# A two-layer decoder trunk in single-pass float32: part of the second MLP product as seven block products for eight

## The chip, the cores and the metric

One core of a Trainium2 chip runs the kernel. The metric is the device time of one execution in microseconds (us), the median of the runs shown. The program before takes 853.79 us.

## What is computed

The reference is a decoder trunk of two layers on 256 tokens of width 1024. Each layer has a mixer (sparse attention and retention), a squared-ReLU MLP and a gated embedding. What the change touches is the MLP:

```
h = rmsnorm(x, norm_mlp[i])
x = x + jnp.square(jax.nn.relu(h @ w_ff1[i])) @ w_ff2[i]
gate = jax.nn.sigmoid(rmsnorm(x, norm_ple[i]) @ w_ple_gate[i])
x = x + gate * (p[i] @ w_ple[i])
```

`w_ff1` is 1024 x 4096 and `w_ff2` is 4096 x 1024.

## The kernel before

The residual stays on the chip as `XT`, features on partitions, tokens along the free axis (8 chunks of 128 features x 256 tokens). Every float32 product is made of three TensorE passes on float32r operands: each operand is split in a rounded part ("high") and the remainder ("low"), and high x high, high x low and low x high are added in PSUM (`three`, L485).

Weights come in units of 128 x 1024 (512 KB). `PLAN` (`_plan`, L71) is the order of units; `take` (L360) hands out the next one and has `advance` (L331) start loads on the SP queue and splits four units ahead. A split (`unit_split`, L312) is one rounding copy on ScalarE (`hi`) and one subtraction on VectorE (`lo`); there are six `hi` and six `lo` buffers (`HL`), so a unit's split waits until TensorE is through with the unit six places before it. TensorE's order is that of the code; ScalarE's, VectorE's and the SP queue's is made by a scheduler from dependences and priorities. Each of these queues runs in order.

The MLP of a layer (L1078 to L1135) works in 16 pairs of contraction tiles, 256 rows of the hidden width each. For a pair `i`, the first product (`ff1_unit`, `b_unit`, L490) takes two units, weights stationary and 256 tokens moving: 48 matmuls of 256 columns into one PSUM tile of the pool `mm` (three banks, L122). `ff1_end` (L1089) makes Relu, its square twice (one rounded, for the high part) and the remainder: two ScalarE and two VectorE instructions of 512 columns. Two pairs later the second product (`ff2`, L1103, with `wide`, L509) takes two units of `w_ff2`, weights stationary again: 2 tiles x 8 output blocks x 3 passes = 48 matmuls of 256 columns into four PSUM accumulators (pools `sc` and `pt`, two banks each). The norm's factor `r` is left out of the MLP's input; its square, spread over partitions by two flips (`finish_b`, L469), multiplies the sums at the end (L1132), which are then added to `XT` and fed to the next stage (`feed`, L454: `XH` on ScalarE, `XL` on VectorE, squares for the norm).

After the MLP comes the product `ple` (two units, 24 matmuls each of 256 columns for two halves), which needs nothing of the MLP, and then the gate product (`gate`), which needs `XH` and `XL`.

A flip (`flip`, L222) is a 128 x 128 transposition on TensorE against an identity.

Of the kernel before, what the change touches and what calls it, by code (L numbers as in the profile page):

```python
# [70 lines left out]
def _plan(l):  # L71
    r = [({"w": "w1"}.get(n, n), u) for n, u in SEQ[l] if n not in ("fa", "fb", "sq")]
    for n in ("ma", "mb"):
        r += [(n, u) for u in range(8)]
    r += [("ua", u) for u in range(4)] + [("ub", 0), ("ub", 1), ("ub", 2), ("out", 0), ("out", 1)]
    r += [("ub", 3)] + [("out", u) for u in range(2, 8)]
    r += [("ff1", u) for u in (0, 2, 1, 3)]
    for i in range(14):
        r += [("ff1", 2 * i + 4), ("ff1", 2 * i + 5), ("ff2", 2 * i), ("ff2", 2 * i + 1)]
    r += [("ff2", u) for u in range(28, 32)]  # L80
# [7 lines left out]
BIG_UNITS = [x for x in PLAN if x[1] != "kvg"]  # L88
# [6 lines left out]
def trunk(ctx: ExitStack, tc: tile.TileContext, xT, wu, wg, cst, msk, par, pin, out):  # L95
# [25 lines left out]
    def mm_tile(shape):  # L121
        return ps.tile(shape, F32, tag="mm", name=nm("mm"), bufs=3)  # L122
# [16 lines left out]
    def big(shape, tag, name, dt=F32):  # L139
        return bp.tile(shape, dt, tag=tag, name=nm(name))  # L140
# [39 lines left out]
    def fresh(t=None):  # L180
        cur[0] = vt["pe"] if t is None else t
# [107 lines left out]
    state = {"load": 0, "split": 0, "take": 0}  # L289
    raws, his, los, spans, due = {}, {}, {}, {}, {}  # L290

    def unit_load(i):
        key = PLAN[i]
        if key[1] == "w1":
            t = bp.tile([P, NW], F32, tag=f"B{(1, 2, 5, 6)[key[2] % 4]}", name=f"raw{i}")
        else:
            t = wp.tile([P, NW], F32, tag="raw", name=f"raw{i}", bufs=RAW)
        if key[1] == "kvg":
            nc.sync.dma_start(t[:, :560], wg[KVG_IX[key]])
            spans[i] = 560  # L300
        else:
            src = wu[BIG_IX[key]]
            if i == 0:
                for c in range(4):
                    load_x(c, c + 1)
                    nc.sync.dma_start(t[:, c * 256:(c + 1) * 256], src[:, c * 256:(c + 1) * 256])
            else:
                nc.sync.dma_start(t, src)
            spans[i] = NW
        raws[i] = t  # L310

    def unit_split(i, ahead=None):  # L312
# [12 lines left out]
        due[i] = cur[0]

    ring = [0]
    for key in PLAN:
        ring.append(ring[-1] + (key[1] != "w1"))

    def advance(i):  # L331
        n = len(PLAN)
# [189 lines left out]
    def layer(l, st):  # L522
# [550 lines left out]
        ph = big([P, 2, S], "S7", "ph", F32R)  # L1073
        pl = big([P, 2, S], "S8", "pl", F32R)
        act(ph, pT, AF.Copy)
        sub(pl, pT, ph.bitcast(F32))

        def ff1_unit(i, u):  # L1078
            if u == 0:
                ff[i] = mm_tile([P, 2, S])  # L1080
            b_unit(ff[i], take(l, "ff1", 2 * i + u), XH, XL, 4 * u, u == 0, u == 1)
            if u == 1:
                ff1_end(i, ff[i])

        def ff1(i):
            for u in range(2):
                ff1_unit(i, u)

        def ff1_end(i, pm):  # L1089
            fresh()  # L1090
            au = big([P, 2, 2, S], f"B{i % 3}", "au")
            ho = big([P, 2, 2, S], f"B{3 + i % 4}", "ho", F32R)
            a, u2 = au[:, 0], au[:, 1]
            h, o = ho[:, 0], ho[:, 1]
            act(a, pm, AF.Relu)
            tt(out=h, in0=a, in1=a, op=ALU.mult)
            act(u2, a, AF.Square)
            sub(o, u2, h.bitcast(F32))
            ff[i] = (h, o)

        pf = []

        def ff2(i):  # L1103
            h, o = ff.pop(i)
            for u in range(2):
                w = take(l, "ff2", 2 * i + u)
                if not pf:
                    pf.extend(accumulators())
                for n in range(4):
                    wide(pf[n], w, n, h[:, u, :], o[:, u, :], i == 0 and u == 0, False)  # L1110

        ff1_unit(0, 0)
        ff1_unit(1, 0)
        ff1_unit(0, 1)
        ff1_unit(1, 1)
        finish_a(stf)
        ff1(2)
        finish_b(stf, square=True)
        ff2(0)
        for i in range(1, 14):  # L1120
            ff1(i + 2)
            ff2(i)
        ff2(14)
        stp = new_stage(l, 2)
        ws = [take(l, "ff2", 30 + u) for u in range(2)]
        dz = [big([P, 2, 2, S], f"B{1 + i}", "dz") for i in range(2)]
        h, o = ff.pop(15)
        for n in range(4):
            for u in range(2):
                wide(pf[n], ws[u], n, h[:, u, :], o[:, u, :], False, u == 1)  # L1130
            d = dz[n // 2][:, n % 2]
            tt(out=d, in0=pf[n], in1=bc2(stf["RB"]), op=ALU.mult)  # L1132
            xc = XT[:, 2 * n:2 * n + 2, :]
            tt(out=xc, in0=xc, in1=d, op=ALU.add)
            feed(stp, 2 * n)  # L1135
# [108 lines left out]
def _unit(l, name, u, a):  # L1244
# [27 lines left out]
        return bform(a["w_up_ret"][l], 256 * u, 0, 4)  # L1272
    if name == "out":
        return a["w_out"][l][u * P:(u + 1) * P]
    if name == "ff1":
        return bform(a["w_ff1"][l], 256 * (u // 2), 4 * (u % 2), 4)
    if name == "ff2":
        return a["w_ff2"][l][u * P:(u + 1) * P]
    if name == "gate":
# [45 lines left out]
```

## Time and profile before

| | |
|---|---|
| median of three runs | 853.79 us (853.41 to 854.06) |
| the profiled execution | 853.69 us, span 851.9 us |
| TensorE busy | 840.6 us, 99% |
| VectorE busy | 605.1 us, 71% |
| ScalarE busy | 499.8 us, 59% |
| GpSimd busy | 77.5 us, 9% |
| bytes moved | 152.11 MB, mean 179 GB/s |

The span runs from the first to the last instruction of the profiled execution; the device time is 1.8 us more. Busy times of engines overlap. Matmuls are pipelined: one takes longer from its start to its modelled end than the next one's start is away.

### The profile page before, as it was taken

What the parts mean: (1) busy time and instruction counts of PE and PEld (TensorE: products, weight loads), DVE (VectorE), ACT (ScalarE), POOL (GpSimd) and SP (SyncE); (2) the same over time, 40 slices, a digit from 0 to 9 for tenths busy, and PEclk for the clock granted to TensorE, in tenths of its full rate; (3) what the DMA queues carried; (4) which work ended last, traced back from release to release, by engine and by line L of the source; (5) the groups of instructions that cost most, each with busy time, mean ns of one, the idle gap of its engine ahead of it and who ended that gap; (6) DMA issues with size and microseconds to landing.
All of it is one profiled execution on the core that took longest, in us unless ns stands there. A gap on an engine that the chain in (4) does not pass through costs nothing.

```text
span 851.9 us, 16528 instructions
## 1 busy us (share of the span) xinstructions
PE 840.6 (99%) x6647; PEld 816.6 (96%) x6647; DVE 605.1 (71%) x977; ACT 499.8 (59%) x836; POOL 77.5 (9%) x68
## 2 busy tenths in 40 slices
PE   8999999999999999999999999999999999999997
PEld 7988899999999999999999989999999999999997
DVE  6897897786955555557789979886877555555584
ACT  6786877544744545445567768765465444444471
POOL 1240241000000000000004104120000000000000
PEclk9999999999999999999999999999999999999999
DMA  8877454356565655556655664443546556656541
GB/s 262 311 243 242 127 154 126 121 166 188 175 185 187 180 191 179 192 180 221 200 193 158 218 198 141 133 138 121 175 149 216 181 189 183 189 183 187 185 124 50
DMA packets 44284, 152.11 MB, mean 179 GB/s; under 512 B 5168, under 2 KB 6960, under 8 KB 44208
## 3 DMA queue, kind: packets, MB, share of 16 engines
q1 hardware_dynamic: 44064, 151.04, 55.9%
q8 instruction: 52, 0.85, 0.4%
q14 instruction: 24, 0.20, 0.1%
q10 hardware_dynamic: 144, 0.01, 0.0%
HBM read 149.99 MB, written 1.05 MB: 177 GB/s over the span
## 4 chain that ended last, share of the span: by engine, by line
PE 89%; DVE 6%; DMA 1%; ACT 1%; issue 1%; POOL 1%; SPq 0%; DVEq 0%; ACTq 0%
PE mm L220 51%; PE sc L220 18%; PE pt L220 14%; PE ot L220 4%; PE pt L225 2%; DVE lo L192 2%; DMA raw<-in_wu_dram 1%; POOL rso L214 1%; DVE tmp L200 0%; ACT hi L188 0%; DVE zt L192 0%; ACT tmp L188 0%; DVE yss L204 0%; DVE T L200 0%; DVE zs L192 0%
## 5 line engine op out<-in xcount | busy, mean ns | idle before, releaser
L192 DVE TENSOR_TENSOR lo<-raw,hi 128x1024 fp32r<-128x1024 f32 (+2 forms) x287 | 347.6, 1217 | 185.7 <-ACT hi L188 184.9
L188 ACT ACTIVATE hi<-raw 128x1024 fp32r<-128x1024 f32 (+2 forms) x287 | 296.5, 1039 | 276.6 <-PE mm L220 158.7
L220 PE MATMUL mm<-XH,hi 128*128 128x256 f32 x992 | 283.5, 286 | 0.0
L220 PE MATMUL mm<-XH,lo 128*128 128x256 f32 x992 | 279.6, 282 | 0.0
L220 PE MATMUL mm<-XL,hi 128*128 128x256 f32 x992 | 279.1, 281 | 0.0
L220 PEld LDWEIGHTS mm<-XH,hi 128*128 128x128 f32 x992 | 187.0, 188 | 2.0
L220 PEld LDWEIGHTS mm<-XL,hi 128*128 128x128 f32 x992 | 187.0, 189 | 1.7
L220 PEld LDWEIGHTS mm<-XH,lo 128*128 128x128 f32 x992 | 186.8, 188 | 0.0
L220 PE MATMUL sc<-ho,hi 128*128 128x256 f32 x512 | 96.8, 282 | 0.0
L220 PE MATMUL pt<-ho,hi 128*128 128x256 f32 x512 | 96.6, 281 | 0.0
L220 PEld LDWEIGHTS pt<-ho,hi 128*128 128x128 f32 x512 | 78.6, 188 | 0.0
L220 PEld LDWEIGHTS sc<-ho,hi 128*128 128x128 f32 x512 | 78.5, 188 | 0.0
L220 PE MATMUL pt<-ho,lo 128*128 128x256 f32 x256 | 72.0, 281 | 0.0
L220 PE MATMUL sc<-ho,lo 128*128 128x256 f32 x256 | 72.0, 281 | 0.0
L220 PEld LDWEIGHTS sc<-ho,lo 128*128 128x128 f32 x256 | 48.2, 188 | 0.0
L220 PEld LDWEIGHTS pt<-ho,lo 128*128 128x128 f32 x256 | 48.2, 188 | 0.0
L214 POOL TENSOR_TENSOR e<-e,acf 128x512 f32<-128x512 f32 (+1 forms) x32 | 37.3, 1194 | 113.4 <-DVE acf L192 76.0
L220 PE MATMUL mm<-hi,XH 128*128 128x512 f32 (+2 forms) x128 | 44.3, 346 | 0.0
L220 PE MATMUL mm<-lo,XH 128*128 128x512 f32 (+2 forms) x128 | 43.7, 342 | 0.1
L220 PE MATMUL mm<-hi,XL 128*128 128x512 f32 (+2 forms) x128 | 43.7, 341 | 0.0
L188 ACT ACTIVATE e<-e,nmx 128x128 f32<-128x128 f32 (+2 forms) x96 | 37.6, 394 | 7.4 <-DVE nmx L208 7.4
L214 POOL TENSOR_TENSOR r<-ms,mhalf 128x2 f32<-128x2 f32 x6 | 6.6, 1100 | 365.2 <-DVE ms L196 337.0
(192 smaller groups left out, 1362.7 us busy)
## 6 DMA issues: line engine op xcount, KB each, us to landing
raw<-in_wu_dram SPq DMA_DIRECT2D x275, 512.0 KB, 3.7
raw<-in_wg_dram SPq DMA_DIRECT2D x8, 280.0 KB, 4.2
cst<-in_cst_dram SPq DMA_DIRECT2D x1, 768.0 KB, 7.0
out_dram<-XT SPq DMA_DIRECT2D x3, 256.0 KB, 2.4
XT<-in_xT_dram SPq DMA_DIRECT2D x4, 128.0 KB, 2.8
raw<-in_wu_dram SPq DMA_DIRECT2D x4, 128.0 KB, 2.8
XT<-in_xT_dram SPq DMA_DIRECT2D x2, 256.0 KB, 5.9
tmp<-in_pin_dram SPq DMA_DIRECT2D x2, 256.0 KB, 3.8
```

What stands on the lines that cost most here:

```text
L188: return nc.scalar.activation(o, *a, **k)
L192: return nc.vector.tensor_tensor(**k)
L214: return nc.gpsimd.tensor_tensor(**k)
L220: return nc.tensor.matmul(o, a, b_, **k)
L225: return nc.tensor.transpose(o, a, i)
```

## The change

The hidden activations of a pair are now seen as a 2 x 2 block matrix (two token tiles, two contraction tiles), the two units of `w_ff2` as 2 x 2 blocks of 128 x 512. In 6 of 16 pairs (`PLAIN`) the product stays eight block products; in ten it is made of seven (Winograd's form). Activations (`ah`, `al`) are stationary, 128 x 128, and weights move, 512 columns a matmul, so sums come out with tokens on partitions.

For the ten pairs both raw units are loaded into one tile (`pair_load`), VectorE makes sums of weight blocks (`pair_part`), and the split is in four parts (`s2a` to `s2d`, the last half as wide): 3.5 splits for 2. `ff1` units now cover 128 hidden rows with all of the contraction; four units at the start keep the old form under the name `fh`. `ff1_end` works by 256 columns, makes the sums of activation blocks, and splits 768 (plain) or 896 columns. Seven accumulators hold what the products add to: two in pool `mm` (numbers 1 and 6), two in `sc`, two in `pt`, one in `ot`. After the last seven-product pair (`LAST`) and in the last pair they are joined in single VectorE passes that also multiply by the squared norm factor `r2`, now one number per token and so per partition. `turn_back` then flips the result 128 x 128 wise and adds it to `XT`. `ph` and `pl` move to a pool of their own.

```diff
+PAIR = ("s2a", "s2b", "s2c", "s2d")
+PLAIN = (0, 3, 6, 9, 12, 15)
...
+    r += [("fh", u) for u in (0, 2, 1, 3)]
+    for i in range(16):
+        x = [("ff2", 2 * i), ("ff2", 2 * i + 1)] if i in PLAIN else [(n, i) for n in PAIR]
+        m = len(x) // 2
+        a, b = ([("ff1", 2 * i + 4)], [("ff1", 2 * i + 5)]) if i < 14 else ([], [])
+        r += a + x[:m] + b + x[m:]
...
+    def pair_load(l, i):
+        j = sum(k not in PLAIN for k in range(i))
+        B = bp.tile([P, 2, 2, 512], F32, tag=(f"S{2 * l + 1}", f"S{2 * l + 2}", "S7")[j % 3], name="pair")
+        for k in range(2):
+            nc.sync.dma_start(B[:, k].rearrange("p a b -> p (a b)"), wu[BIG_IX[(l, "ff2", 2 * i + k)]])
+        T = bp.tile([P, 3, 512], F32, tag=f"S{5 + j % 2}", name="tsum")
+        pairs[l, i] = B, T
+
+    def pair_part(l, n, i):
+        B, T = pairs[l, i]
+        if n == "s2a":
+            tt(out=T[:, 0:2], in0=B[:, :, 1], in1=B[:, 0], op=ALU.subtract)
+            return B[:, :, 0]
+        if n == "s2b":
+            sub(T[:, 2], B[:, 1, 1], T[:, 0])
+            sub(B[:, 0, 1], B[:, 1, 0], T[:, 2])
+            return T[:, 0:2]
+        if n == "s2c":
+            return B[:, :, 1]
+        pairs.pop((l, i))
+        return T[:, 2:3]
...
+        def ff1_end(n, pm):
+            i, u = n // 2, n % 2
...
+            act(a, pm, AF.Relu)
+            act(a, a, AF.Square)
+            if i in PLAIN:
+                if u == 0:
+                    return
+                v = A[:, 0:4].rearrange("p (k t) q -> p k t q", t=2)
+                sub(A[:, 4:6], v[:, :, 1], v[:, :, 0])
+                used = A[:, 0:6]
+            else:
+                if u == 0:
+                    sub(A[:, 6], A[:, 1], A[:, 0])
+                    return
+                tt(out=A[:, 4], in0=A[:, 0], in1=A[:, 2], op=ALU.add)
+                sub(A[:, 5], A[:, 4], A[:, 1])
+                sub(A[:, 7], A[:, 3], A[:, 5])
+                used = A[:, 1:8]
+            m = used.shape[1]
+            h = big([P, m, P], f"B{1 + 2 * (i % 3)}", "ah", F32R)
+            o = big([P, m, P], f"B{2 + 2 * (i % 3)}", "al", F32R)
+            act(h, used, AF.Copy)
+            sub(o, used, h.bitcast(F32))
...
+        PROD = {"s2a": ((1, 0, 0), (2, 2, 1)), "s2b": ((5, 3, 0), (7, 5, 1)),
+                "s2c": ((4, 1, 0), (3, 6, 1)), "s2d": ((6, 4, 0),)}
+        def product(i, m, j, w, b, last=False):
+            h, o = ff[i]
+            c = 512 * b
+            three(pf[m], h[:, j], o[:, j], w[0][:, c:c + 512], w[1][:, c:c + 512], m not in begun, last)
...
+        def grow(o, m, t, base):
+            stt(out=o, in0=pf[m], scalar=r2[:, t:t + 1], in1=base, op0=ALU.mult, op1=ALU.add)
...
         finish_a(stf)
-        finish_b(stf, square=True)
+        r2 = small([P, 2], "r2")
+        tt(out=r2, in0=stf["r"], in1=stf["r"], op=ALU.mult)
+        for i in range(15):
+            for half in range(2):
+                if i < 14:
+                    ff1(2 * i + 4 + half)
+                ff2(i, half)
...
+        def turn_back(n):
+            for j in range(2):
+                pt = (s_tile, p_tile)[j]([P, 2, S])
+                for q in range(2):
+                    for t in range(2):
+                        c = (2 * j + q) * P
+                        flip(pt[:, q, t * P:(t + 1) * P], yo[n][:, t, c:c + P], ident)
+                c = 4 * n + 2 * j
+                xc = XT[:, c:c + 2, :]
+                with tc.high_priority():
+                    tt(out=xc, in0=xc, in1=pt, op=ALU.add)
+                    feed_x(stp, c, 2)
+                feed_sq(stp, c, 2)
+
+        for m, j, b, ends in ((2, 1, 0, ((yo[0][:, 1], 1, v[1]),)), (4, 0, 0, ((yo[0][:, 0], 0, v[0]),)),
+                              (5, 0, 1, ((yo[1][:, 0], 0, v[0]), (u1, 1, u1))),
+                              (3, 4, 1, ((yo[1][:, 1], 1, u1),))):
...
+            if m == 5:
+                turn_back(0)
...
+                if u == 0 and n == 1:
+                    turn_back(1)
```

Three places of the new order bear on the prediction. The first is VectorE at the start of layer 0's MLP. Before, from the last `lo` of the early first-product units on (`ho` are the split activations, `ms` belongs to the norm):

```order
L192 TENSOR_TENSOR lo_2836<-raw_2736,hi_2835 128x1024
L192 TENSOR_TENSOR lo_2880<-raw_2767,hi_2879 128x1024
L192 TENSOR_TENSOR ho_2828<-au_2827 128x512
L192 TENSOR_TENSOR ho_2828<-au_2827,ho_2828 128x512
L196 TENSOR_SCALAR ms_2872<-pt_2869 128x2
L192 TENSOR_TENSOR lo_2910<-raw_2797,hi_2909 128x1024
L192 TENSOR_TENSOR ho_2864<-au_2863 128x512
```

The same place now (`aq` are squared activations, `tsum` and `pair` the weight sums, `r_267` is `r2`, `al` the remainders that the second product needs):

```order
L203 TENSOR_TENSOR lo_2845<-raw_2740,hi_2844 128x1024
L203 TENSOR_TENSOR tsum<-pair 128x1024
L203 TENSOR_TENSOR lo_2897<-raw_2770,hi_2896 128x1024
L203 TENSOR_TENSOR aq_2834<-aq_2834 128x256
L203 TENSOR_TENSOR tsum<-pair,tsum 128x512
L207 TENSOR_SCALAR ms_2888<-pt_2885 128x2
L203 TENSOR_TENSOR pair<-pair,tsum 128x512
L203 TENSOR_TENSOR r_267_2892<-r_2890 128x2
L203 TENSOR_TENSOR lo_2939<-pair,hi_2938 128x1024
L203 TENSOR_TENSOR al_2841<-aq_2834,ah_2840 128x768
```

Three weight sums of the second seven-product pair and `r2` have come in ahead of pair 0's `al`, and `r2` follows `ms` by one instruction.

The second place is ScalarE in the middle of the MLP, one seven-product pair (`aq<-mm` is the Relu that empties a PSUM bank of the first product, `aq<-aq` the square):

```order
L199 ACTIVATE hi_3405<-raw_3247 128x1024
L199 ACTIVATE aq_3390<-mm_3365 128x256
L199 ACTIVATE aq_3390<-aq_3390 128x256
L199 ACTIVATE hi_3417<-pair 128x1024
L199 ACTIVATE hi_3456<-tsum 128x1024
L199 ACTIVATE hi_3468<-raw_3343 128x1024
L199 ACTIVATE aq_3390<-mm_3422 128x256
L199 ACTIVATE aq_3390<-aq_3390 128x256
L199 ACTIVATE hi_3477<-pair 128x1024
L199 ACTIVATE hi_3510<-tsum 128x512
L199 ACTIVATE ah_3450<-aq_3390 128x768
```

Before, a pair had four `hi`, one Relu and one square of 512 columns; each Relu now stands right behind the `hi` that waits for the same first-product unit.

The third place is TensorE at the end of the MLP, from the third of the last four products on:

```order
L231 MATMUL sc_2930<-hi_4525,al_4491 128x512
L236 MATMUL sc_4597<-cst,yo_4573 128x128 x4
L236 MATMUL pt_4609<-cst,yo_4573 128x128 x4
L231 MATMUL pt_2932<-hi_4511,ah_4490 128x512
L231 MATMUL pt_2932<-lo_4512,ah_4490 128x512
L231 MATMUL pt_2932<-hi_4511,al_4491 128x512
```

Eight flips stand between the third and the last product, and eight more between the two halves of `ple`; before, the last product was followed by `ple` without a flip.

## Rows read from the trace of the kernel before

**Rows 1.** The page: busy time by engine, and the chain's shares.

```profile
PE 840.6 (99%) x6647; PEld 816.6 (96%) x6647; DVE 605.1 (71%) x977; ACT 499.8 (59%) x836; POOL 77.5 (9%) x68
...
PE 89%; DVE 6%; DMA 1%; ACT 1%; issue 1%; POOL 1%; SPq 0%; DVEq 0%; ACTq 0%
```

**Rows 2.** The page: busy tenths in 40 slices, VectorE and granted clock.

```profile
DVE 6897897786955555557789979886877555555584
...
PEclk9999999999999999999999999999999999999999
```

**Rows 3.** Busy time in three stretches, with instruction counts, granted clock and DMA.

```profile
core 0: us, PE busy (x) PEld busy (x) DVE busy (x) ACT busy (x) POOL busy (x), PEclk, DMA share, GB/s
75.70:81.20 5.50, 5.50 (x25) 4.36 (x24) 4.19 (x5) 3.14 (x4) 0.00 (x0) 1.00 0.47 147
150.00:163.00 13.00, 13.00 (x108) 12.60 (x107) 9.24 (x12) 6.27 (x9) 0.56 (x1) 1.00 0.42 125
228.15:399.30 171.15, 171.15 (x1444) 171.15 (x1444) 95.57 (x97) 81.15 (x94) 1.65 (x2) 1.00 0.61 192
```

**Rows 4.** Timeline of TensorE, first and last of 24 wide matmuls: start, us, engine.

```profile
75.76 0.40 PE L220 MATMUL mm<-hi,XH 128*128 128x512 f32 x1
...
81.12 0.40 PE L220 MATMUL mm<-hi,XL 128*128 128x512 f32 x1
```

**Rows 5.** Timeline of TensorE, flips in attention and in the MLP.

```profile
140.34 0.60 PE L225 MATMUL pt<-cst,e 128*128 128x128 f32 x4
...
233.93 0.38 PE L225 MATMUL pt<-cst,r 128*128 128x128 f32 x2
```

**Rows 6.** Groups by shape, 150 to 163 us: flips, busy us and mean ns.

```profile
L225 PE MATMUL pt<-cst,e 128*128 128x128 f32 x16 | 2.4, 272 | 0.0
```

**Rows 7.** Groups by shape in 100 us of the MLP (260 to 360 us).

```profile
L192 DVE TENSOR_TENSOR lo<-raw,hi 128x1024 fp32r<-128x1024 f32 x35 | 42.9, 1226 | 44.2 <-ACT hi L188 44.2
...
L188 ACT ACTIVATE hi<-raw 128x1024 fp32r<-128x1024 f32 x36 | 38.2, 1062 | 54.0 <-PE mm L220 32.2 <-PE pt L220 21.8
...
L192 DVE TENSOR_TENSOR ho<-au,ho 128x512 fp32r<-128x512 f32 x9 | 6.2, 692 | 0.9
```

**Rows 8.** Groups by shape over the whole span: small instructions.

```profile
L192 DVE TENSOR_TENSOR z<-z 128x256 f32<-128x256 f32 x6 | 2.5, 416 | 0.0
...
L200 DVE SCALAR_TENSOR_TENSOR tmp<-tmp,rso,rG 128x128 f32<-128x128 f32 x16 | 4.6, 347 | 3.3 <-POOL rso L214 3.3
...
L188 ACT ACTIVATE RB<-pt 128x256 f32<-128x256 f32 x6 | 2.3, 381 | 7.7 <-PE pt L225 7.7
```

**Rows 9.** Timeline of VectorE, instructions back to back behind the MLP.

```profile
399.95 0.68 DVE L192 TENSOR_TENSOR dz<-pt,RB 128x512 f32<-128x512 f32 x1
400.55 0.87 DVE L200 SCALAR_TENSOR_TENSOR XL<-XT,par,XH 128x256 fp32r<-128x256 f32 x2
...
409.67 2.36 DVE L192 TENSOR_TENSOR lo<-raw,hi 128x1024 fp32r<-128x1024 f32 x2
```

**Rows 10.** Timeline at the start of layer 0's MLP; last, all six of GpSimd's powers.

```profile
223.63 2.35 DVE L192 TENSOR_TENSOR lo<-raw,hi 128x1024 fp32r<-128x1024 f32 x2
...
228.15 0.37 PE L220 MATMUL mm<-XH,hi 128*128 128x256 f32 x1
...
228.63 0.15 DVE L196 TENSOR_SCALAR ms<-pt 128x2 f32<-128x2 f32 x1
...
228.86 0.69 POOL L214 TENSOR_TENSOR r<-ms,mhalf 128x2 f32<-128x2 f32 x1 [52.42 <-DVE ms L196]
...
L214 POOL TENSOR_TENSOR r<-ms,mhalf x6: 695/990/1625, 22.7 to 835.6; 128x2 f32<-128x2 f32 x6
```

**Rows 11.** Timeline in the MLP: a first-product unit ends, `hi` and Relu follow.

```profile
302.50 0.40 PE L220 MATMUL sc<-ho,hi 128*128 128x256 f32 x2
302.59 1.06 ACT L188 ACTIVATE hi<-raw 128x1024 fp32r<-128x1024 f32 x1 [1.79 <-PE mm L220]
...
303.56 0.58 ACT L188 ACTIVATE au<-mm 128x512 f32<-128x512 f32 x1
```

More of the change, by code (lines that the diff above doesn't have):

```diff
@@ L87 @@
     PLAN += _plan(_l)
-BIG_UNITS = [x for x in PLAN if x[1] != "kvg"]
+BIG_UNITS = []
+for _x in PLAN:
+    if _x[1] == "s2a":
+        BIG_UNITS += [(_x[0], "ff2", 2 * _x[2] + _j) for _j in range(2)]
+    elif _x[1] != "kvg" and _x[1] not in PAIR:
+        BIG_UNITS.append(_x)
 BIG_IX = {x: i for i, x in enumerate(BIG_UNITS)}
@@ L328, in trunk @@
     for key in PLAN:
-        ring.append(ring[-1] + (key[1] != "w1"))
+        ring.append(ring[-1] + (key[1] != "w1" and key[1] not in PAIR))
     def advance(i):
@@ L1085, in ff1, with ff1_mm @@
[L1085 to L1089, printed above, removed]
+        def ff1_mm(pm, w, k0):
+            vh = w[0].rearrange("p (k n) -> p k n", k=8)
+            vl = w[1].rearrange("p (k n) -> p k n", k=8)
+            for k in range(k0, k0 + 4):
+                three(pm, vh[:, k], vl[:, k], XH[:, k, :], XL[:, k, :], k == 0, k == 7)
+        def ff1_end(n, pm):
+            i, u = n // 2, n % 2
+            if u == 0:
+                ff[i] = big([P, 8, P], ("B0", "S8")[i % 2], "aq")
+            A = ff[i]
+            a = A[:, 2 * u:2 * u + 2].rearrange("p a b -> p (a b)")
@@ new lines, in ff2 @@
+        def ff2(i, half):
+            if not pf:
+                accumulators_of(7, 5, 4, 3, 2)
+            if i in PLAIN:
+                w = take(l, "ff2", 2 * i + half)
+                for m, j, b in ((2, 1 + 2 * half, 0), (4, 2 * half, 0), (5, 2 * half, 1), (3, 4 + half, 1)):
+                    product(i, m, j, w, b)
+                return
+            if 1 not in pf:
+                accumulators_of(1, 6)
+            for n in PAIR[2 * half:2 * half + 2]:
+                w = take(l, n, i)
+                for m, j, b in PROD[n]:
+                    product(i, m, j, w, b, i == LAST and m in (1, 6, 7))
+                    if i == LAST and m in (1, 6, 7):
+                        combine(m)
@@ new lines, in layer @@
+        pms = [mm_tile([P, 2, S]) for _ in range(2)]
+        for u in range(2):
+            for i in range(2):
+                b_unit(pms[i], take(l, "fh", 2 * i + u), XH, XL, 4 * u, u == 0, u == 1)
+                if u == 1:
+                    for q in range(2):
+                        ff1_end(2 * i + q, pms[i][:, q])
+        finish_a(stf)
+        r2 = small([P, 2], "r2")
[5 more added lines that the diff above has]
+                ff2(i, half)
@@ L1124, in layer @@
         stp = new_stage(l, 2)
         ws = [take(l, "ff2", 30 + u) for u in range(2)]
-        dz = [big([P, 2, 2, S], f"B{1 + i}", "dz") for i in range(2)]
-        h, o = ff.pop(15)
-        for n in range(4):
-            for u in range(2):
[L1130 to L1135, printed above, removed]
+        yo = [big([P, 2, 512], f"B{3 + n}", "yo") for n in range(2)]
@@ new lines, in layer @@
+        for m, j, b, ends in ((2, 1, 0, ((yo[0][:, 1], 1, v[1]),)), (4, 0, 0, ((yo[0][:, 0], 0, v[0]),)),
+                              (5, 0, 1, ((yo[1][:, 0], 0, v[0]), (u1, 1, u1))),
+                              (3, 4, 1, ((yo[1][:, 1], 1, u1),))):
+            for u in range(2):
+                product(15, m, j + (u if m == 3 else 2 * u), ws[u], b, u == 1)
+            fresh()
+            with tc.high_priority():
+                for o, t, base in ends:
+                    grow(o, m, t, base)
+            if m == 5:
+                turn_back(0)
```

88 lines of the change are left out of this document (48 added, 40 removed).

## The prediction

> **What bounds the kernel now.** I read the page first: TensorE is busy 99% of the span and makes 89% of the chain that ended last [rows 1]. Next the slices: VectorE works at five to nine tenths, and it is at five tenths over most of the two MLP stretches; the granted clock is at its top everywhere [rows 2]. So an edit pays if it takes time from TensorE's stream, and as long as VectorE, ScalarE or the loads don't come late instead. A busy TensorE is not TensorE at its peak, so what a matmul costs is read from how far apart matmuls stand. In layer 0's MLP, 1444 matmuls of 256 columns fill 171.15 us: 118.5 ns each, with no gap [rows 3]. Of 512 columns, 24 in a row start from 75.76 to 81.12 us, so 23 steps take 5.36 us: 233 ns each, while VectorE was busy 4.19 of 5.5 us [rows 3, 4]. Two narrow ones cost 237 ns, one wide one 233.
>
> **The change, part by part, per layer.** *Second product.* Before: 16 pairs x 2 tiles x 8 output blocks x 3 passes = 768 matmuls of 256 columns, 768 x 118.5 = 91.0 us. After: six plain pairs of 24 and ten of 21 (7 block products x 3 passes), 354 matmuls of 512 columns, 354 x 233 = 82.5 us. Gain 8.5 us. If a wide one cost just two narrow ones (237 ns) the gain would be 7.1. The number of matmuls in the first product stays, each 256 columns.
> The Trainium skill gives N/2.4 + 2.5 ns between matmuls (TensorE: Matmul & The Clock Gate, "Back-to-back issue gap"). By it the product would go from 768 x 109.2 = 83.8 to 354 x 215.8 = 76.4 us, a gain of 7.5; the rows show 118.5 and 233, so both of its prices are too low here and the sum goes by the rows.
> *Turning back.* Sums now have tokens on partitions, so 16 flips of 128x128 per layer are new. Four flips take 0.60 us with 0.272 us for the last to end, so a step is 0.11 us [rows 5, 6]: 16 x 0.11 = 1.75 us on the path. Gone are the two flips that spread the squared norm [rows 5]: 0.2 us. Net on TensorE: 8.5 - 1.75 + 0.2 = 7.0 us a layer, 14.0 us for two.
>
> *VectorE and ScalarE in the middle.* In the MLP a 1024-column `lo` takes 1.23 us, a 1024-column `hi` 1.06, a 512-column subtraction 0.69 [rows 7]; 256 columns take 0.42 on VectorE and 0.38 on ScalarE, 128 columns 0.35 [rows 8]; 768 and 896 columns lie between, 0.96 and 1.1 on VectorE. A seven-product pair costs VectorE six 1024s (two first-product `lo`, the pair sum, three `lo`), three 512s, four 128s and one 896: 7.4 + 2.1 + 1.4 + 1.1 = 12.0 us, against 48 x 0.1185 + 21 x 0.233 = 10.6 us on TensorE. There VectorE is over. A plain pair costs it 4 x 1.23 + 0.42 + 0.96 = 6.3 us against 48 x 0.1185 + 24 x 0.233 = 11.3. Two of one kind and one of the other: 30.3 us of VectorE in 32.5 of TensorE, 93%; back to back its instructions stand closer than they last (512 columns 0.60, 1024 columns 1.14 [rows 9]), which makes it about 27, 84%. The shortfall of two seven-product pairs in a row is at most 2 x 1.4 = 2.8 us. Six `hi`/`lo` buffers let the splits run five units ahead, and the shortest five units in a row are 7.7 us of TensorE (three of 6 x 0.233, one of 3 x 0.233, one of 24 x 0.1185). So the lead swallows the shortfall and the plain pair restores it: I cost the middle at nothing. If that cover were gone, 1.4 us in each of 20 pairs would be 28 us. ScalarE: 5 x 1.06 + 0.6 + 4 x 0.4 + 0.95 = 8.5 us a pair, less than TensorE's 10.6. The loads are the same bytes; a pair is fetched up to 11 units ahead, and the SP queue waits for nothing that isn't released in the same order.
>
> *Start of the MLP.* Here a wait is added: `r2` on VectorE needs GpSimd's power, and behind it stand a `lo` and `al` of pair 0, which the third matmul of the first second-product unit waits for. In this trace VectorE is through its fourth early `lo` at 226.0, the first-product unit before that point starts at 228.15, `ms` at 228.63, GpSimd at 228.86 [rows 10]. With the new order: one 512 (the `ph`/`pl` split, now earlier) leaves and the pair sum of 1.14 comes: 226.5; `lo` 227.7; 256 columns 228.0; 512 228.6; `ms` 228.8; 512 229.4; `r` lands GpSimd's 0.69 to 1.63 after about 229.0 [rows 10]; `r2` 229.9 to 230.8; `lo` +1.1; `al` +0.96: 232.0 to 232.9. It is needed at 228.15 + 24 x 0.1185 + 2 x 0.233 = 231.5. A stall of 0.4 to 1.4 us; I take 0.7, for GpSimd's median of 0.99. Two layers: 1.4.
> *End of the MLP.* Count from the end of the third last product. TensorE then does 8 flips (0.87), the last product (1.40), half of `ple` (2.84), 8 flips, the other half: the gate product starts at 8.8. ScalarE's queue has a `hi` whose buffer the last product frees, so the first `XH` comes at 3.9; VectorE stands at its `XL` until 4.3, then makes the last `yo` at 4.9 (flips at 5.1: in time), three `XL` (0.44 each [rows 9]) paced by ScalarE, two sums on the flips (7.4), two `XL`, and in layer 0 only then the gate's `lo`, at 9.8, where 9.1 is wanted. 0.7 us once; in layer 1 that `lo` stands before the `XL`. The accumulators' eight reads replace four, in the shadow of products.
> **Sum.** 14.0 - 1.4 - 0.7 = 11.9 us off. The profiled execution took 853.69 us (span 851.9), 0.1 below the median of 853.79: 853.7 - 11.9 = **841.8 us**.
>
> **Rivals.**
> *A, edges dear.* Each wait at the two edges ends later: GpSimd at its longest and the whole queue behind it (1.4), and at the end all four chunks behind ScalarE's blocked `hi` (2.4 more). Some 3.8 us a layer instead of 1.05: 841.8 + 5.5 = 847.3. For it: both edges hold chains over three engines. Against: the same edges have no gap now.
> *B, one bank (slower).* Seven of the eight PSUM banks hold sums once the first seven-product pair starts, so first-product units share one, and each must wait until ScalarE's Relu has emptied it. Relu stands in ScalarE's queue behind one `hi` that waits for the same unit: `hi` starts 0.1 after TensorE turns to the next tile, Relu 0.97 later [rows 11], and takes 0.38 [rows 8]: done at 1.45. The next first-product unit comes after 9 x 0.233 = 2.1 us at the narrowest, so it is in time by 0.6. Were a second and third `hi` late before it (+1.9), each of 8 narrow places a layer would lose 1.25 us and each of 18 wide ones (2.8) 0.55: 20 us a layer, 853.7 - 11.9 + 40 = 882 us. It decides the sign when a first-product unit loses 0.21 us on average (11.9 us over 56 units). The Trainium skill names the sign to look for (Perfetto Trace Analysis, "Identifying the Most-Contended Engine"): the same gap repeated on the engine that should be full can mean too little PSUM or SBUF.
> *C, VectorE bound.* If waits for `hi` cost VectorE over 4 us in each three pairs, it needs more than the 3 x 96 x 0.1185 = 34.1 us that three pairs take now, and the product gains nothing while flips and edges stay: 853.7 + 3.1 + 2.1 = 858.9 us. Now it waits for `hi` 44 us in 100, but all of it where ScalarE waits for TensorE to free a buffer [rows 7], which is no loss.
> *D, clock.* In the 13 us with 20 flips the granted clock stayed 1.00 [rows 3]. The Trainium skill says that transposes don't count as work for the clock (TensorE: Matmul & The Clock Gate, "Part 4: PE-mode transpose"), and the row disagrees for groups of four; groups of eight no row shows. If the clock fell to its half level behind each of four groups, 6 x 0.233 + 24 x 0.1185 = 4.2 us would take as long again: 17 us, 858.6 us.
>
> **Chances.** Forecast 0.66 (838 to 844.5), A 0.18, B 0.06, C 0.04, D 0.01, and 0.05 that the edges and repeated small gaps eat it to within 0.2%. Range: without any stall and with wide matmuls at 229 ns it is 853.7 - 14.0 - 2.8 = 837; A with its margin reaches 848.5. Below the range 0.05, above it 0.15. A measurement of this kernel can tell about 0.2%, 1.7 us. Faster by more than that: forecast, A, part of B, 0.87; within 0.05; slower 0.08.
>
> **What would show it.** Right: second-product matmuls 230 to 235 ns apart, 354 a layer; no TensorE gap inside pairs 1 to 14; one gap under 1.5 us a layer where the first `al` is awaited; flips in fours of 0.60. Wrong: a gap of equal size before first-product units, ended by ScalarE (B); VectorE near 100% in the MLP with TensorE waiting for `lo` (C); the clock row under 9 behind flips (D); gaps of over 2 us before the gate (A).

## The result and the profile after

The changed kernel took 844.63 us (median of 4 runs, 842.08 to 845.54) beside 853.91 for the kernel before (4 runs, 853.41 to 854.06): a ratio of 0.9886, 95% interval 0.9874 to 0.9898. That is 9.3 us less and inside the stated range (837 to 848.5), but just above the 844.5 up to which the prediction counted the forecast, and about as far from its sum, 841.8, as from rival A's 847.3. So the number alone does not choose between the two; the stretches below do. Run again, the changed kernel took 841.4 to 844.9: its runs spread over 4 us where those of before spread over less than 2, and this turns out to be part of the answer.

The page of the changed kernel (profiled run 844.83 us) answers to [rows 1, 2]:

```profile
span 842.8 us, 15192 instructions
...
PE 827.7 (98%) x5847; PEld 770.3 (91%) x5847; DVE 702.3 (83%) x1147; ACT 563.6 (67%) x974; POOL 77.7 (9%) x68
...
DVE  6898798787988978978879978886979888889695
...
PEclk9999999999999999999999999999999999999999
...
PE 82%; DVE 10%; DMA 2%; ACT 2%; issue 2%; POOL 1%; SPq 1%; DVEq 0%; ACTq 0%; POOLq 0%
```

VectorE, at five tenths in the MLP before, stands at seven to nine there. The clock holds. TensorE's part of the chain fell from 89% to 82%: there are waits now. Where they are is read by cutting the span at matmuls that both kernels have (starts on TensorE's timeline; "norm" is the first matmul with the tile `ones` behind the gate's first products):

| stretch, us | before | after | saved | forecast |
|---|---|---|---|---|
| start to end of layer 0's output product | 216.15 | 216.22 | -0.07 | 0 |
| to the gate's norm, layer 0 (MLP) | 200.28 | 195.30 | 4.98 | 5.6 |
| to end of layer 1's output product | 218.13 | 220.10 | -1.97 | 0 |
| to the gate's norm, layer 1 (MLP) | 200.22 | 194.08 | 6.14 | 6.3 |
| to the end | 17.12 | 17.12 | 0.00 | 0 |

The two MLP stretches gave 11.1 of the 11.9 us forecast. Then 2.0 us were lost in a stretch that the change does not touch, where I had costed nothing.

**Start of the MLP.** The timeline of the changed kernel (TensorE, VectorE and GpSimd at the first second-product unit; compare [rows 10]):

```profile
228.61 0.15 DVE L207 TENSOR_SCALAR ms<-pt 128x2 f32<-128x2 f32 x1
...
228.84 1.13 POOL L225 TENSOR_TENSOR r<-ms,mhalf 128x2 f32<-128x2 f32 x1 [51.96 <-DVE ms L207]
230.01 0.16 DVE L203 TENSOR_TENSOR r<-r 128x2 f32<-128x2 f32 x1 [0.59 <-POOL r L225]
230.09 1.22 DVE L203 TENSOR_TENSOR lo<-pair,hi 128x1024 fp32r<-128x1024 f32 x1
...
231.22 0.95 DVE L203 TENSOR_TENSOR al<-aq,ah 128x768 fp32r<-128x768 f32 x1
231.29 0.40 PE L231 MATMUL ot<-lo,ah 128*128 128x512 f32 x1
...
232.23 0.50 PE L231 MATMUL ot<-hi,al 128*128 128x512 f32 x1 [0.55 <-DVE al L203]
```

VectorE stands idle for GpSimd's power, squares it (`r2`, shown as `r<-r`), and only then makes `lo` and `al`. The third matmul starts 0.94 us after the second instead of 0.23: a gap of 0.71 us, 0.74 in layer 1.

**End of layer 0's MLP.** Same kernel, ScalarE, VectorE and TensorE:

```profile
393.09 1.06 ACT L199 ACTIVATE hi<-raw 128x1024 fp32r<-128x1024 f32 x1 [1.43 <-DMA raw<-in_wu_dram]
394.06 0.89 ACT L199 ACTIVATE XH<-XT,par 128x256 fp32r<-128x256 f32 x2
...
394.58 0.48 DVE L211 SCALAR_TENSOR_TENSOR XL<-XT,par,XH 128x256 fp32r<-128x256 f32 x1 [1.27 <-ACT XH L199]
394.98 0.75 DVE L211 SCALAR_TENSOR_TENSOR yo<-pt,r,tmp 128x512 f32<-128x512 f32 x1
...
395.17 0.27 PE L236 MATMUL sc<-cst,yo 128*128 128x128 f32 x1
395.79 0.55 PE L236 MATMUL sc<-cst,yo 128*128 128x128 f32 x3 [0.34 <-DVE yo L211]
...
398.99 1.22 DVE L203 TENSOR_TENSOR lo<-raw,hi 128x1024 fp32r<-128x1024 f32 x1
...
400.26 0.39 PE L231 MATMUL mm<-XH,lo 128*128 128x256 f32 x1 [0.40 <-DVE lo L203]
```

Two gaps: 0.51 us inside a group of flips, because the last `yo` stands behind an `XL` that waits for `XH`, which stands behind a `hi` that waits for its load; and 0.56 before the gate's `lo`. In layer 1 there is none.

**Layer change.** The timeline of the changed kernel where the stretch lost its 2 us (ScalarE, VectorE, GpSimd, TensorE):

```profile
438.98 1.06 ACT L199 ACTIVATE hi<-raw 128x1024 fp32r<-128x1024 f32 x1 [3.41 <-PE mm L231]
440.07 1.23 DVE L203 TENSOR_TENSOR lo<-raw,hi 128x1024 fp32r<-128x1024 f32 x1 [3.25 <-ACT hi L199]
441.21 0.15 DVE L207 TENSOR_SCALAR ms<-pt 128x2 f32<-128x2 f32 x1
...
441.51 0.70 POOL L225 TENSOR_TENSOR r<-ms,mhalf 128x2 f32<-128x2 f32 x1 [27.20 <-DVE ms L207]
...
442.26 0.43 PE L236 MATMUL pt<-cst,r 128*128 128x128 f32 x2 [0.55 <-POOL r L225]
```

`ms` stands behind a `lo`, that `lo` behind ScalarE's `hi`, and that `hi` starts when its load has landed, at 438.87 (the row names TensorE, which had long been done). In the kernel before, `r` was there 1.2 us before the flips that spread it were due, and they followed without a gap; now `ms` comes 1.9 us later, and the gap is 0.74 us. Three smaller gaps in the 22 us behind it make the other 1.2 us of the stretch. The list of DMA issues for that one load, of the changed kernel and then of the kernel before:

```profile
raw<-in_wu_dram SPq DMA_DIRECT2D x1, 512.0 KB, 6.2
```

```profile
raw<-in_wu_dram SPq DMA_DIRECT2D x1, 512.0 KB, 4.4
```

It took 6.2 us from issue to landing instead of 4.4. Over the whole span the waits of ScalarE's `hi` for loads grew, in the list of waits of before and of after (us in total, times, longest):

```profile
ACT hi L188 <- DMA raw<-in_wu_dram: 17.5, 16, 2.2
```

```profile
ACT hi L199 <- DMA raw<-in_wu_dram: 28.9, 27, 3.2
```

### The profile page after: what moved, and what is told of

Same layout as the page of the kernel before. It is cut to its first block, busy times and chain, and to the rows that moved or that the text cites. A ratio compares the mean times of both kernels' runs of the same rounds, so it can differ in the third digit from the quotient of the medians.

```text
span 842.8 us, 15192 instructions
## 1 busy us (share of the span) xinstructions
PE 827.7 (98%) x5847; PEld 770.3 (91%) x5847; DVE 702.3 (83%) x1147; ACT 563.6 (67%) x974; POOL 77.7 (9%) x68
## 4 chain that ended last, share of the span: by engine, by line
PE 82%; DVE 10%; DMA 2%; ACT 2%; issue 2%; POOL 1%; SPq 1%; DVEq 0%; ACTq 0%; POOLq 0%
PE mm L231 51%; PE sc L231 12%; PE pt L231 10%; PE ot L231 7%; DVE lo L203 4%; PE pt L236 2%; DMA raw<-in_wu_dram 2%; POOL rso L225 1%; DVE zt L203 1%; ACT hi L199 1%; DVE zs L203 0%; ACT XH L199 0%; DVE tsum L203 0%; DMA tmp<-in_pin_dram 0%; DVE tmp L211 0%
## 5 line engine op out<-in xcount | busy, mean ns | idle before, releaser
L199 ACT ACTIVATE hi<-raw 128x1024 fp32r<-128x1024 f32 (+2 forms) x247 | 253.7, 1034 | 163.2 <-PE mm L231 99.8
L203 DVE TENSOR_TENSOR lo<-raw,hi 128x1024 fp32r<-128x1024 f32 (+2 forms) x247 | 297.7, 1216 | 55.1 <-ACT hi L199 52.8
L203 DVE TENSOR_TENSOR lo<-pair,hi 128x1024 fp32r<-128x1024 f32 x40 | 48.9, 1223 | 17.8 <-ACT hi L199 16.9
L199 ACT ACTIVATE hi<-pair 128x1024 fp32r<-128x1024 f32 x40 | 42.1, 1052 | 20.3 <-PE mm L231 19.9
L199 ACT ACTIVATE hi<-tsum 128x1024 fp32r<-128x1024 f32 (+1 forms) x40 | 33.6, 840 | 16.7 <-PE pt L231 11.3
L203 DVE TENSOR_TENSOR lo<-tsum,hi 128x1024 fp32r<-128x1024 f32 (+1 forms) x40 | 38.2, 954 | 7.0 <-ACT hi L199 7.0
L225 POOL TENSOR_TENSOR rso<-rsv,mhalf 128x2 f32<-128x2 f32 (+3 forms) x18 | 26.7, 1488 | 122.4 <-DVE rsv L207 122.4
L203 DVE TENSOR_TENSOR al<-aq,ah 128x896 fp32r<-128x896 f32 (+1 forms) x32 | 33.2, 1038 | 2.3 <-ACT ah L199 2.0
L231 PE MATMUL pt<-hi,ah 128*128 128x512 f32 x88 | 34.8, 395 | 0.0
L231 PE MATMUL pt<-hi,al 128*128 128x512 f32 x88 | 34.7, 395 | 0.0
```

The source lines that it names most:

```text
L199: return nc.scalar.activation(o, *a, **k)
L203: return nc.vector.tensor_tensor(**k)
L225: return nc.gpsimd.tensor_tensor(**k)
L231: return nc.tensor.matmul(o, a, b_, **k)
```

## The experiments

All but before_raw5 start from the changed kernel. Times are medians; the ratio is to the kernel before on the same chip.

**1. The same kernel again (again, again2).** No edit.

> The changed kernel once more, nothing edited, for a second profile. In the first one, 9.1 us came of the 11.9 forecast: 4.98 in layer 0's MLP, 6.14 in layer 1's, and 1.97 were given back between the `ones` of layer 0's gate and the end of layer 1's output product, where ScalarE's `hi` waited for loads that took 5.8 to 6.2 us from issue to landing instead of 4.4 to 5.0. Theory 1: those loads were late in that execution only. Then the stretch takes 218.1 to 219 us here (220.10 in the first profile, 218.13 before the change), and the total of this execution is nearer 842 than 844.8. Theory 2: the change itself makes them late. Then the same gap of 0.7 us in front of the spread of the row statistics comes back, the stretch takes 220 us again, and the runs lie at 844 to 845.

> The changed kernel a third time, for one more profile. Its eight runs so far lie at 841.4 to 842.1 us (three) and at 844.4 to 845.5 (five), and both profiles so far were of the upper kind. Theory 1 (the lower runs are those in which the layer change has no late load): a profile near 842 shows the loads of that stretch at 4 to 5 us, no gap there, and 218 us between layer 0's gate and the end of layer 1's output product. Theory 2 (the 3 us lie elsewhere): the stretch is 220 us at either time.

Measured: 843.13 us (841.37 to 844.86; ratio 0.9873, 0.9854 to 0.9891), profiled run 844.79; and a single run of 843.06. In the first, the stretch between the layers took 220.68 us and the same load 6.4 us, with the gap before `pt<-cst,r` again, which was theory 2's sign. In the second the stretch took 218.84 us and that gap was gone, with the load at 4.7:

```profile
raw<-in_wu_dram SPq DMA_DIRECT2D x1, 512.0 KB, 4.7
```

Of the 1.8 us between these two runs, 0.88 is that gap and 0.56 two smaller ones in the 18 us behind it; the other 0.4 lies behind the attention. So 1.4 us goes with that one load being late or not: theory 1, for this part. But slow loads there are not chance alone. That load is the first of four issued within 5 us, and the third of the four took 5.6 to 6.7 us in all eleven profiles of kernels with seven-product pairs (6.0 in again2 too), against 4.5 to 5.0 in the three without (before, before_raw5, all_plain). No profile fell on a run near 841.4, so what the fastest runs save on top stays unseen. The first stretch alone took 215.25 and 215.76 us here, up to a us less than in the first profile; 0.6 and 0.1 us of that lie in gaps of its first 18 us.

**2. The square out of the way (late_r2).**

```diff
-        tt(out=r2, in0=stf["r"], in1=stf["r"], op=ALU.mult)
         for i in range(15):
+            if i == 2:
+                tt(out=r2, in0=stf["r"], in1=stf["r"], op=ALU.mult)
```

> The square `r2` is taken two pairs later, so VectorE's queue no longer stands behind GpSimd's power before pair 0's `lo` and `al`. Theory 1 (the wait for `r2` is the start stall): `lo` starts 0.67 us earlier (229.4 instead of 230.09 in layer 0), `al` ends at 231.5 where it is needed at 231.5, the gap of 0.71 us before the third matmul of pair 0 goes to under 0.1 in both layers, and the time falls by 1.3 us against the changed kernel. Theory 2 (VectorE is the real limit of the MLP and the stall only gives it lead): the gap goes, but gaps of the same sum come behind it in pairs 1 to 14, and the time stays within 0.3 us. Theory 3 (ScalarE's `hi` and `ah` are just as late): the gap shrinks by less than 0.3.

Measured: 841.98 us (ratio 0.9858, 0.9845 to 0.9872). The timeline at the place of the gap:

```profile
229.32 1.22 DVE L203 TENSOR_TENSOR lo<-pair,hi 128x1024 fp32r<-128x1024 f32 x1
230.45 0.95 DVE L203 TENSOR_TENSOR al<-aq,ah 128x768 fp32r<-128x768 f32 x1
...
231.23 0.40 PE L231 MATMUL ot<-lo,ah 128*128 128x512 f32 x1
231.46 0.49 PE L231 MATMUL ot<-hi,al 128*128 128x512 f32 x1
```

The gap is gone in both layers and none comes behind it in pairs 1 to 14: the MLP stretches are 194.35 and 193.37 us, 0.95 and 0.71 less. That is theory 1 by the trace. The medians, 843.13 for the unedited kernel on the same chip, show 1.2 less; alone they would not settle it, since late loads move them by more than that.

**3. No seven-product pair (all_plain).** `PLAIN = tuple(range(16))`, and the four results scaled by `r2` without a base.

> All 16 pairs with eight block products; activations stationary, single passes and the turning back stay, and the accumulators of the seven-product form with their ScalarE reads are gone. Theory 1 (the gain is TensorE's, term by term): 20 pairs get three more matmuls of 233 ns each, 14.0 us on top of the changed kernel, some 858.6 us: slower than before the change, by the flips (1.75 a layer) and the start stall less the 1.5 a layer that wide matmuls save. VectorE's share falls by about a fifth of the MLP. Theory 2 (VectorE costs the changed kernel something hidden): the lighter VectorE gives part of it back, and the time is under 857. Theory 3 (wide and single-pass form is worth something by itself, beyond 233 against 237 ns): 853 or less.

Measured: 854.12 us (ratio 1.000, 0.9991 to 1.0009): wide matmuls with the sums turned back are worth next to nothing by themselves (0.6 us in each MLP stretch, given back outside the MLP), and the gain is the eighth product saved in ten pairs. But it is 4.5 us faster than the 858.6 of theory 1. The trace has the rest: the MLP stretches are 199.67 us each, 9.96 more in sum than in the first profile of after, not 14.0. Both start stalls are gone (1.45), and so is the end loss in layer 0 (1.23, from the last second-product matmul to the gate's norm). The remaining 1.3 us is pace: second-product matmuls followed each other at 232.1 instead of 232.9 ns (of late_r2, which has no start stall), first-product ones at 118.5 instead of 119.1. VectorE was busy 66 of 120 us here (third pair of numbers):

```profile
260.00:380.00 120.00, 120.00 (x769) 108.78 (x769) 65.95 (x66) 68.16 (x97) 0.00 (x0) 1.00 0.58 186
```

The time is theory 2's: the seven-product form costs some 4 us beside its matmuls, two thirds of it at edges. That VectorE's load is the cause is shown only in part: the start stall is a wait in VectorE's queue (experiment 2), the end loss went with earlier loads (experiment 7), and on the pace nothing was tried.

**4. Fourteen seven-product pairs (seven14).**

```diff
-PLAIN = (0, 3, 6, 9, 12, 15)
+PLAIN = (0, 15)
```

> Fourteen pairs instead of ten as seven block products (pairs 1 to 14, plain ones only 0 and 15), nothing else. Theory 1 (VectorE takes what its instructions take back to back, about 10.8 us a pair against 10.6 of TensorE, and the lead covers the 0.2): eight more pairs save 0.70 us each, 5.6 us, some 839 us, with no TensorE gap in the MLP. Theory 2 (VectorE needs the sum of its durations, 12.0 us a pair): from the fifth or sixth pair in a row TensorE waits 1.4 us in each, up to 12 us a layer, and the time is 855 to 863. Between the two: VectorE's idle time and the first pair in which TensorE waits tell the true cost of a pair on VectorE.

Measured: 837.37 us (ratio 0.9804, 0.9790 to 0.9817), no gap in the MLP but the one at the start and, at the end of layer 0, the two of the changed kernel (0.46 and 0.56 us). One window in it, of the changed kernel and of this one:

```profile
260.00:360.00 100.00, 100.00 (x646) 90.93 (x645) 85.31 (x107) 68.58 (x98) 0.00 (x0) 1.00 0.55 186
```

```profile
260.00:360.00 100.00, 100.00 (x654) 91.28 (x653) 99.55 (x134) 71.35 (x104) 0.00 (x0) 1.00 0.59 194
```

VectorE is busy 99.55 of 100 us (third pair of numbers) and TensorE does not wait. A pair takes TensorE 48 x 0.119 + 21 x 0.233 = 10.6 us, so VectorE, busy 99.55% of that time, takes some 10.55 us for it (experiment 5 gives 10.4): the sum of durations, 12.0, was the wrong bound, the back-to-back one the right one.

**5. Where VectorE ends (vector_plus).** Edit, on the fourteen-pair kernel: the first line of `pair_part` twice.

> The fourteen-pair kernel with the pair sum (`T[:, 0:2]`, 1024 columns) taken twice in each seven-product pair: VectorE gets 1.14 us more a pair, back to back. From the fourteen-pair trace VectorE needs at most 10.55 us a pair against TensorE's 10.61, so it would be 1.08 over. Theory 1 (it was at its limit and the splits run up to five units, 7.7 us, ahead): 14 x 1.08 = 15.1 us of shortfall a layer, less the lead, 7.4 us: 837.4 + 14.8 = 852 us, with TensorE's first wait for `lo` about seven pairs in. Theory 2 (the lead was already used up): no pair is covered, 837.4 + 30 = 867 us. Theory 3 (VectorE had slack that its busy time hides): 838 to 841 us.

Measured: 854.62 us (ratio 1.0004). The window shows VectorE without a break, and the timeline TensorE's first gap of the MLP:

```profile
260.00:340.00 80.00, 80.00 (x521) 72.76 (x521) 80.00 (x108) 55.41 (x82) 0.00 (x0) 1.00 0.54 185
```

```profile
348.69 1.24 DVE L203 TENSOR_TENSOR lo<-tsum,hi 128x1024 fp32r<-128x1024 f32 x1
...
348.92 0.39 PE L231 MATMUL sc<-hi,ah 128*128 128x512 f32 x1
...
349.98 0.50 PE L231 MATMUL sc<-lo,ah 128*128 128x512 f32 x1 [0.67 <-DVE lo L203]
```

It comes some ten pairs in, three later than expected, and then once a pair, 0.82 to 0.87 us at first. From the first such wait to the third, a pair takes 11.56 and 11.57 us with VectorE busy without a break; less the 1.14 of the added subtraction that is 10.4 us a pair, under TensorE's 10.6. So the shortfall here is some 0.96 us a pair, and the lead covered about 10 us of it, more than the 7.7 of five units. The MLP stretches grew by 7.65 and 7.99 us, 15.6 together where theory 1 said 14.8; in layer 0 the three steady waits make only 2.5 us of it and three in the last two pairs 4.7, so that the sum agrees is partly luck. The rest of the 17 us is the layer change again (221.01 us there). So the lead is real and is spent: VectorE may run over TensorE for a while, and pays once the lead is used up.

**6. Both edits (both).** Fourteen pairs and the late `r2`.

> Fourteen seven-product pairs and the late `r2` together. Theory 1 (the two act on different things: TensorE's work, and one wait at the start): the start stall of 0.70 us a layer goes as well, 837.4 - 1.4 = 836.0 us. Theory 2 (with VectorE 99.5% busy in the MLP of the fourteen-pair kernel, the stall is what gives VectorE its lead): time saved at the start comes back as waits for `lo` in the last seven-product pairs, 837 us or more.

Measured: 835.90 us (ratio 0.9786, 0.9773 to 0.9800). Theory 1: the start stall goes and comes back nowhere, though VectorE is as full as before.

**7. One more load buffer (raw5, before_raw5).**

```diff
-    RAW = 4
+    RAW = 5
-                    ph = tmp([P, HG, P], F32R, tag="pp", bufs=4)
+                    ph = tmp([P, HG, P], F32R, tag="pp", bufs=2)
```

(and so for every `pp`, to make room.)

> The changed kernel with five instead of four `raw` buffers, so each load can be issued one unit earlier; to make room, the split buffers of the attention (`pp`) are two instead of four, which may cost in the attention stretch and is read apart there. Theory 1 (the 2.0 to 2.6 us lost between layer 0's gate and layer 1's output product, in two profiles of the changed kernel, are ScalarE's waits for loads): the waits of `hi` for `raw` there shrink by over a unit, the gap before the spread of the row statistics goes, and the stretch from layer 0's gate `ones` to layer 1's attention takes 89 us as before the change instead of 90.2. Theory 2 (the loads are limited by what the queue moves, not by buffers): the waits stay and the stretch is unchanged.

> The kernel before the change with five `raw` and two `pp` buffers: how much of that gain has nothing to do with the change. Theory 1 (the first stretch and the attention gain as in the changed kernel, the MLP and the layer change had no stall before): 1.3 us at the start and 0.5 at layer 1's attention, some 852.3 us. Theory 2 (the late loads are of the change alone): 853.7 to 854.2, no difference.

Measured: the changed kernel 839.70 us (839.52 to 839.84; ratio 0.9831, 0.9818 to 0.9844), the kernel before 851.54 (851.23 to 853.11; ratio 0.9974, 0.9964 to 0.9983). The waits of `hi` for loads, changed kernel and then the one before:

```profile
ACT hi L199 <- DMA raw<-in_wu_dram: 8.5, 9, 2.6
```

```profile
ACT hi L188 <- DMA raw<-in_wu_dram: 6.1, 7, 1.8
```

From layer 0's gate to layer 1's attention it is 87.75 us in both, where the first profile of after had 90.28 and the kernel before 88.32; the first stretch is 214.87 and 214.67; and in layer 0's MLP both end gaps of the changed kernel went (195.30 to 194.01 us). So they hung on late loads as well, and for the changed kernel it is theory 1; the kernel before gained more than theory 1's 852.3. What two `pp` buffers instead of four do by themselves was not tried. With five buffers in both, the change is worth 851.54 - 839.70 = 11.84 us (two chips, on which the kernel before took 854.17 and 854.22).

**8. All together (best), and a fifteenth pair (seven15).** Fourteen pairs, late `r2`, five buffers; then `PLAIN = (15,)`.

> Fourteen seven-product pairs, late `r2`, and five `raw` buffers with two `pp` buffers. Five `raw` buffers took 3.4 us off the changed kernel (843.1 to 839.7): 0.9 to 1.3 us in the first stretch, 1.3 at the end of layer 0's MLP, and the rest at the layer change. Theory 1 (they act on loads, not on VectorE): the fourteen-pair kernel with the late `r2` has 0.4 us of stall left at the end of layer 0's MLP and 0.4 to 0.8 at the layer change, so it gains 0.4 + 0.6 + 1.2 = 2.2 us: 833.7 us. Theory 2 (the gain was the same 3.4 whatever the MLP): 832.5.

> As the kernel named best here, with pair 0 as seven block products too: 15 pairs. TensorE saves 0.70 us a layer more, 1.4. Theory 1 (the start has no time for it): pair 0's `al` needs four more VectorE instructions (three sums of 128 columns and 896 instead of 768 columns) and its third sum before the first second-product unit, at least 1 us, while the start has no slack now: a stall of 0.7 us or more a layer gives it back, and the time is 833.5 to 835. Theory 2 (the earlier matmuls hide it): 832.3.

Measured: 832.37 us (ratio 0.9745, 0.9732 to 0.9759), the fastest of all, 22 us under the kernel before. The parts add up: from fourteen pairs alone the late `r2` took off 1.5 us (837.37 to 835.90) and the buffers 3.5 more, as much as from the changed kernel, which is theory 2; the first stretch gave 1.4 of it (216.13 to 214.77), the layer change 1.25, layer 0's MLP 0.6. Its page has TensorE back at 91% of the chain:

```profile
PE 820.7 (99%) x5823; PEld 765.9 (92%) x5823; DVE 733.7 (88%) x1211; ACT 570.2 (69%) x990; POOL 78.8 (9%) x68
...
PE 91%; DVE 5%; ACT 1%; DMA 1%; issue 1%; POOL 0%; SPq 0%; DVEq 0%
```

The fifteenth pair gives nothing: 832.53 us. Its three matmuls less (0.70 us a layer) come back as 0.60 and 0.62 us where the first `al` is awaited. That is theory 1's mechanism; the time is under its 833.5 because the kernel that it starts from was 1.3 us faster than the 833.7 it was worked out from.

**9. The one bank (bank_late).** On the kernel with five buffers, each Relu behind the first four is repeated four times.

```diff
             act(a, pm, AF.Relu)
+            if n >= 4:
+                with tc.high_priority():
+                    for _ in range(4):
+                        nc.scalar.activation(a, pm, AF.Relu)
```

> The kernel with five `raw` buffers, with each of the 56 Relus after the first four done five times in a row (same result): the first product's only free PSUM bank is handed back 4 x 0.27 = 1.08 us later (two Relus back to back take 0.64 us, one 0.37). In that kernel's trace the next first-product unit starts 0.67 to 0.69 us after the Relu's end at 16 narrow places and 1.2 to 1.4 us after it at most others. Theory 1 (rival B's mechanism, with its slack as measured): 0.4 us lost at each narrow place, none at the others, 839.7 + 6.4 = 846.1 us, and equal TensorE gaps ended by ScalarE before first-product units. Theory 2 (the delay feeds on itself: ScalarE's `hi` behind the Relus come late and the next Relu with them): every one of 56 places loses, 855 us or more. Theory 3 (the bank does not bind): 840.

Measured: 950.96 us (ratio 1.1124). The delay was more than I wrote: the repeated Relus write one tile and start 0.41 us apart, not 0.27, and at 36 of the 56 places the scheduler set two `hi`s between them:

```profile
264.85 0.36 ACT L199 ACTIVATE aq<-mm 128x256 f32<-128x256 f32 x1
265.24 0.38 ACT L1151 ACTIVATE aq<-mm 128x256 f32<-128x256 f32 x1
265.65 1.06 ACT L199 ACTIVATE hi<-raw 128x1024 fp32r<-128x1024 f32 x1
266.61 0.36 ACT L1151 ACTIVATE aq<-mm 128x256 f32<-128x256 f32 x1
266.88 1.05 ACT L199 ACTIVATE hi<-pair 128x1024 fp32r<-128x1024 f32 x1
267.82 0.79 ACT L1151 ACTIVATE aq<-mm 128x256 f32<-128x256 f32 x2
```

```profile
265.92 0.40 PE L231 MATMUL mm<-hi,al 128*128 128x512 f32 x1
268.67 0.39 PE L231 MATMUL mm<-XH,hi 128*128 128x256 f32 x1 [2.35 <-ACT aq L1151]
```

The bank came free at 268.61 instead of 265.21. TensorE waited 2.0 to 2.65 us at such places and 0.35 where the Relus stood together (4 x 0.41 = 1.64 us late, less a slack of 1.2 to 1.4): delay less slack, as in theory 1, but of a larger delay and at 47 of the 56 places, so that the time is of theory 2's kind. The Trainium skill says that the same gap repeated on the engine that should be full can mean too little PSUM (Perfetto Trace Analysis, "Optimization Strategy"; the prediction names the section before it); here it is one bank, and the rows agree. It had a second price. Behind some of these waits TensorE ran at half its clock for a while, windows of 355 to 360 us:

```profile
355.40:356.40 1.00, 0.99 (x8) 1.00 (x9) 0.97 (x3) 0.40 (x1) 0.00 (x0) 1.00 0.70 258
356.45:359.80 3.35, 3.35 (x18) 3.35 (x17) 1.39 (x3) 0.95 (x1) 0.00 (x0) 0.50 0.42 146
```

Granted 0.50, that is 1.2 GHz, and the 256-column matmuls there start 0.21 us apart instead of 0.12.

## Why the forecast was right, and where it was not

**Second product: right.** In late_r2, which has no start stall to blur it, 354 matmuls at 232.9 ns make 82.4 us; before, 768 at 118.8 made 91.2. Gain 8.8 where I took 8.5. My 118.5 was a little low: of the 1444 matmuls counted in that window two had started before it and two are flips. What I did not have is the first product's pace, 118.7 before and 119.1 after: 672 x 0.4 ns = 0.27 us a layer. The formula that I took from the Trainium skill (TensorE: Matmul & The Clock Gate, "Back-to-back issue gap") stands there as the gap of a single matmul, beside a sustained figure of 131 ns for 512 columns. The rows, at 233 ns, agree with neither that nor the formula's 215.8.

**Turning back: right.** Seven steps between flips took 0.76 us, 0.109 each. Eight in a row left the granted clock at 1.00, so rival D had no ground. The Trainium skill has transposes not counting as work for the clock (TensorE: Matmul & The Clock Gate, "Part 4: PE-mode transpose"); no row here shows them costing clock. Nor does a row test it: the flips here, and the 20 of the prediction's 13 us, stand among other matmuls, so "the row disagrees" went too far.

**Middle at nothing: right, by the lower bound.** No gap in pairs 1 to 14, VectorE at 85% in the window. Experiments 4 and 5 put rival C in its place: VectorE binds when a pair costs it over 10.6 us back to back and more pairs follow than the lead covers. Ten pairs in sixteen was far from that; fourteen, at 10.4 us a pair, come close to it.

**Start stall: right in size and cause.** 0.71 and 0.74 us for 0.7 (0.57 to 0.75 in the next two profiles); experiment 2 takes away the wait alone and the gap goes.

**End stall: half right.** The step that failed is "the last `yo` at 4.9 (flips at 5.1: in time)". The gate's `lo` behind the `XL`s cost 0.56 us as written, but `yo` was late too, and the stretch behind the last second-product matmul took 1.23 us more in layer 0 than in layer 1, not 0.7. I let ScalarE's `hi` wait for a buffer that TensorE frees; it waited for a load, and with five load buffers both gaps went.

**Loads: the step that failed.** "The loads are the same bytes" carried the cost of nothing outside the MLP. The bytes are, but the kernel before already waited for loads at the layer change, with `r` 1.2 us ahead, and the changed kernel came there with a load that took 6.2 and 6.4 us in two of its profiles and 4.7 in a third. The stretch makes 2.0 us of the 2.8 by which the sum missed; the end in layer 0 makes another 0.5. With five buffers in both kernels the change saves 11.84 us, where the sum said 11.9. That is partly luck: the end loss of 0.7 us that the sum takes off is not there then, so it would say 12.6, and the two MLP stretches gave 12.35. Why these transfers are slower stays open: issue time and bytes of the first are the same in all three profiles, the third of that burst is slower in every kernel with seven-product pairs, and I tried nothing that tells causes apart.

**Rivals.** A's place was right in part (layer 0's end) and its size wrong: both edges cost 2.7 us in two layers, where the sum took 2.1 and A 7.6. The time fell near A's for another reason, the loads between the layers. B's mechanism is there, with a slack of 0.67 to 0.69 us at the 16 narrow places where I had worked out 0.6; nothing in the change uses it up, and experiment 9 shows how steeply it costs when something does. That a bank was shared at all cost nothing measurable.

## What to carry to other kernels

When an edit takes work from the engine that bounds, cost the stretches that it does not touch too: where a kernel waits for loads, a transfer that takes 2 us longer can cost as much, and one buffer more in both kernels shows the edit's own worth. For an engine that becomes nearly full, bound its need by how close its instructions follow each other, not by the sum of durations; a lead of some units carries it over the limit for just as long as the lead lasts. A shared PSUM bank cost nothing while its release came early; in experiment 9 what the delay had over the slack was lost at nearly every use.

## What was not expected

- A 512 KB load at one place of the program took 4.4 us in one kernel, and 6.2, 6.4 and 4.7 us in three profiles of another, with the same issue order; the third load of that burst was slower in every kernel with seven-product pairs than in any without.
- VectorE ran at 99.55% over 100 us without holding up TensorE once.
- The pace of TensorE's matmuls rose with VectorE's load: 118.5 to 118.7 ns for 256 columns where VectorE was busy 55% of the time, 119.1 at 85%, 119.2 at 99.5%. No experiment tried why.
- Behind some of the waits of 2.0 to 2.65 us at one bank the granted clock was 0.50, for 3.35 us in the window shown; the mean over the MLP fell to 0.91 to 0.96.
